# Unused columns that shift where the weights lie against the activations in each partition's memory

## The chip, the cores and the metric

The kernel runs on one core of one Trainium2 chip. Time is device time in microseconds (us), the median of three runs. The kernel computes one decoder layer for 256 tokens; nothing is exchanged with other cores.

## The reference, cut to what matters

```python
def hybrid_layer(x, ...):                      # x: (1, 256, 1024) float32
    h = rmsnorm(x, norm_mix_g)
    proj = h @ w_in                            # 1024 -> 3*512 + 512 + 2*1024
    q, k, v, u_pool, gate_logits = jnp.split(proj, ...)
    q = apply_partial_rotary(rmsnorm(heads(q), q_norm_g), pos)
    k = apply_partial_rotary(rmsnorm(heads(k), k_norm_g), pos)
    attn = moba_attention(q, k, heads(v))      # 256 tokens are one block: causal attention, 8 heads of 64
    pooled = multiscale_pool_mixer(u_pool, w_pool, pool_scale)
    gates = jax.nn.sigmoid(gate_logits + b_gate)
    mixed = gates[:, :, 0] * (attn @ w_branch_attn) + gates[:, :, 1] * (pooled @ w_branch_pool)
    x = x + mixed @ w_out
    h2 = rmsnorm(x, norm_ffn_g)
    up = causal_depthwise_conv(h2 @ w_up, conv_w, conv_b)     # 1024 -> 2*2816
    gate, val = jnp.split(up, 2, axis=-1)
    return x + (jax.nn.silu(gate) * val) @ w_down             # 2816 -> 1024
```

## The kernel before, in words

**Three products for one.** Each float32 operand is split into a part rounded to float32r (`hi`, written by `high`, an ACT copy) and the rest (`lo`, written by `low`, a subtraction on DVE, in the feed-forward activations on POOL). Each 128x128 block of a product is then three TensorE matmuls: hi by hi, hi by lo, lo by hi (`mm3`, lines 92 to 94; `down`, lines 640 to 642; `project`, line 283). Every matmul has a stationary operand of 128 columns, which a weight load (PEld) brings in, and a moving operand that is streamed past it.

**Two forms.** From the pooling projection on (`ps_u`, `ps_g`, `ps_m`, `ps_bp`, `ps_ba`, `ps_out`, `ps_up`, `ps_d`) the weights are stationary and the activations, all 256 tokens, are moving: 128x256. In `project`, which makes q, k and v, it is the other way round: 128 tokens of the activations are stationary, and 512 columns of the weights move. The kernel issues 352, 352 and 352 matmuls for `ps_up`, 176 three times for `ps_d`, 128 three times for `ps_g`, 64 three times for `ps_out`, 32 three times each for `ps_u`, `ps_bp` and `ps_ba`, and 4 three times for `ps_m`. Between them stand a few float32 matmuls: transposes (`ps_tq`, `ps_tk`, `ps_p`), scores and values of the attention (`ps_s`, `ps_o`) and the statistics (`ps_n`, lines 243 and 254).

**How the weights come.** `load` brings chunks of 1 MB into four `raw` buffers, on SyncE's queue; `ahead` splits them into four `whi` and four `wlo` buffers some pieces before use; `chunk` hands them to the matmuls. All engines keep the order of the program.

**Where things lie.** A partition's memory is handed out pool after pool: first the constants (pool `const`), then `raw`, `whi`, `wlo`, and then `act`, whose first tile is `xq`: 8 columns of norm weights, then x and the q weights. Behind it in `act` stand `xhi`/`hhi`, `xlo`/`hlo`, `qkT`/`mh`, `vn`/`ml`, `poolh`, `pooll`, `ath` and `atl`, and behind those a pool for temporaries (`ah`, `al`, `u`, `cv` in the feed-forward part). A weight buffer has 8192 bytes in a partition, a stationary slice 512 bytes, a moving slice 1024 bytes (2048 in `project`), so every slice of the weights begins at the same place modulo 512, and every slice of the split activations too. In the built program of before, all of `raw`, `whi` and `wlo` begin at byte 448 modulo 512, and the tiles of `act` behind `xq`, with `ah` and `al`, at 480.

Of the kernel before, what the change touches and what calls it, by code (L numbers as in the profile page):

```python
# [8 lines left out]
F32 = mybir.dt.float32  # L9
# [5 lines left out]
P = 128  # L15
S = 256
NT = S // P
D = 1024
KD = D // P
H = 8  # L20
DH = 64
AW = H * DH
# [30 lines left out]
FFN_AHEAD = 6  # L53
KREADY = 0
FIRST = 2
XCUTS = (1, 2, 4, 6, 8)


@with_exitstack
def hybrid_layer_kernel(ctx: ExitStack, tc: tile.TileContext, xq_d, par_d, wkv_d, wpg_d,  # L60
                        wpool_d, wba_d, wbp_d, wout_d, wup_d, wdn_d, out_d):
    nc = tc.nc

    const = ctx.enter_context(tc.tile_pool(name="const", bufs=1))
# [3 lines left out]
    act = ctx.enter_context(tc.tile_pool(name="act", bufs=1))  # L68
# [109 lines left out]
    nc.vector.memset(ones, 1.0)  # L178


    xq_all = act.tile([P, KD + KD * (S + AW)], F32, name="xq")
    gmix = xq_all[:, 0:KD]
    xq = xq_all[:, KD:].rearrange("p (k c) -> p k c", c=S + AW)
    xT = xq[:, :, 0:S]
# [5 lines left out]
    cut = 0  # L190
    for k in XCUTS:
        end = KD + k * (S + AW)
# [17 lines left out]

    ident = const.tile([P, P], F32, name="ident")
    make_identity(nc, ident)
    mhalf = const.tile([P, H], F32, name="mhalf")
    nc.gpsimd.memset(mhalf, -0.5)
    mask = const.tile([P, 3, P], F32, name="mask")
# [215 lines left out]
    def scores(hp):  # L431
        ps = ps2.tile([P, 2, 512], F32, tag="ps2", name=f"ps_s{hp}")
        for j in range(2):
            rows = slice(j * DH, (j + 1) * DH)
            nc.tensor.matmul(ps[:, j, P:3 * P], qT[rows, hp, P:S], kT[rows, hp, :], start=True, stop=True)
            nc.tensor.matmul(ps[:, j, 0:P], qT[rows, hp, 0:P], kT[rows, hp, 0:P], start=True, stop=True)
        sm = tmp.tile([P, 2, 3 * P], F32, tag="big", bufs=4, name=f"sm{hp}")
        nc.vector.tensor_tensor(sm, ps[:, :, 0:3 * P],
                                mask.rearrange("p a b -> p (a b)")[:, None, :].to_broadcast([P, 2, 3 * P]), ALU.add)
        mx = tmp.tile([P, 2, 2], F32, tag="mx", name=f"mx{hp}")  # L440
        for t in (1, 0):
            nc.vector.tensor_reduce(mx[:, t, :], sm[:, :, TOK[t]], axis=AX.X, op=ALU.max)
        nc.vector.tensor_scalar(mx, mx, -(DH ** -0.5), None, op0=ALU.mult)
        sums = tmp.tile([P, 2, 2], F32, tag="sums", name=f"sums{hp}")
        for j in range(2):
            for t in (1, 0):
                nc.scalar.activation(sm[:, j, TOK[t]], sm[:, j, TOK[t]], AF.Exp, bias=mx[:, t, j:j + 1],
                                     scale=DH ** -0.5, accum_out=sums[:, t, j:j + 1])
        rs = tmp.tile([P, 2, 2], F32, tag="rs", name=f"rs{hp}")
        nc.vector.reciprocal(rs, sums)  # L450
        for t in (1, 0):
            n = TOK[t].stop - TOK[t].start
            nc.gpsimd.tensor_tensor(sm[:, :, TOK[t]], sm[:, :, TOK[t]],
                                    rs[:, t, :, None].to_broadcast([P, 2, n]), ALU.mult)
        later(4, weigh, hp, sm)
# [46 lines left out]
    for n in range(2 * KD):  # L502
        if n >= FIRST and (n - FIRST) % 4 == 0:
            scores((n - FIRST) // 4)
        if n == 10:
# [275 lines left out]
```

## Time and profile before

| what | value |
|---|---|
| median of 3 runs | 347.75 us (347.67 to 347.77) |
| the profiled execution | 347.8 us, of which 346.0 us is the span from the first instruction to the last |
| PE (matmuls) | busy 340.3 us, 98% |
| PEld (weight loads) | 329.3 us, 95% |
| DVE, ACT, POOL | 259.3 us (75%), 198.1 us (57%), 89.4 us (26%) |
| granted TensorE clock, mean | 0.998 |

The span and what lies outside it (1.8 us) make up the execution's time. Matmuls overlap in the records: one is listed with 280 ns, while the next starts 0.11 to 0.12 us after it. The distance from start to start, called the pitch below, is what a matmul costs in a stream of them.

### The profile page before, as it was taken

What the parts mean: (1) busy time and instruction counts of PE and PEld (TensorE: products, weight loads), DVE (VectorE), ACT (ScalarE), POOL (GpSimd) and SP (SyncE); (2) the same over time, 40 slices, a digit from 0 to 9 for tenths busy, and PEclk for the clock granted to TensorE, in tenths of its full rate; (3) what the DMA queues carried; (4) which work ended last, traced back from release to release, by engine and by line L of the source; (5) the groups of instructions that cost most, each with busy time, mean ns of one, the idle gap of its engine ahead of it and who ended that gap; (6) DMA issues with size and microseconds to landing.
All of it is one profiled execution on the core that took longest, in us unless ns stands there. A gap on an engine that the chain in (4) does not pass through costs nothing.

```text
span 346.0 us, 6726 instructions
## 1 busy us (share of the span) xinstructions
PE 340.3 (98%) x2736; PEld 329.3 (95%) x2736; DVE 259.3 (75%) x411; ACT 198.1 (57%) x319; POOL 89.4 (26%) x103
## 2 busy tenths in 40 slices
PE   8999999999999999999999999999999999999995
PEld 7887899999999999999999999999999999999995
DVE  4969889787587585798699977777777777768633
ACT  4956534634748944776467755555556464646420
POOL 1007991112202034123142212121212121221230
PEclk9999999999999999999999999999999999999999
DMA  7985642365272560574257557364646455641003
GB/s 273 421 333 211 217 168 108 150 214 213 86 265 90 230 215 30 172 275 170 116 197 268 183 206 243 122 244 131 236 137 228 145 223 168 209 180 54 0 2 121
DMA packets 10414, 62.76 MB, mean 181 GB/s; under 512 B 1168, under 2 KB 2448, under 8 KB 3472
## 3 DMA queue, kind: packets, MB, share of 16 engines
q1 hardware_dynamic: 10160, 62.01, 49.9%
q8 instruction: 21, 0.34, 0.4%
q10 hardware_dynamic: 224, 0.33, 0.3%
q14 instruction: 9, 0.07, 0.1%
HBM read 61.29 MB, written 1.05 MB: 180 GB/s over the span
## 4 chain that ended last, share of the span: by engine, by line
PE 90%; DMA 5%; DVE 3%; ACT 1%; issue 0%; POOL 0%; SPq 0%; ACTq 0%
PE ps_up L94 12%; PE ps_up L92 12%; PE ps_up L93 12%; PE ps_d L642 6%; PE ps_d L641 6%; PE ps_d L640 6%; PE ps_g L92 5%; PE ps_g L94 4%; PE ps_g L93 4%; DMA raw_k<-in_wkv 3%; PE ps_v L283 3%; PE ps_out L92 2%; PE ps_out L94 2%; PE ps_out L93 2%; PE ps_bp L92 1%; DMA xq<-in_xq 1%
## 5 line engine op out<-in xcount | busy, mean ns | idle before, releaser
L92 PE MATMUL ps_up<-hhi,hi_up 128*128 128x256 f32 x352 | 98.5, 280 | 0.0
L94 PE MATMUL ps_up<-hhi,lo_up 128*128 128x256 f32 x352 | 98.4, 279 | 0.0
L93 PE MATMUL ps_up<-hlo,hi_up 128*128 128x256 f32 x352 | 98.3, 279 | 0.0
L94 PEld LDWEIGHTS ps_up<-hhi,lo_up 128*128 128x128 f32 x352 | 66.2, 188 | 0.2 <-DVE lo_up L84 0.2
L92 PEld LDWEIGHTS ps_up<-hhi,hi_up 128*128 128x128 f32 x352 | 66.2, 188 | 0.0
L93 PEld LDWEIGHTS ps_up<-hlo,hi_up 128*128 128x128 f32 x352 | 66.2, 188 | 0.0
L84 DVE TENSOR_TENSOR lo_up<-raw_up,hi_up 128x1024 fp32r<-128x1024 f32 x44 | 54.5, 1242 | 6.1 <-ACT hi_up L80 6.1
L641 PE MATMUL ps_d<-al,hi_dn 128*128 128x256 f32 x176 | 49.1, 279 | 0.0
L640 PE MATMUL ps_d<-ah,hi_dn 128*128 128x256 f32 x176 | 49.1, 279 | 0.0
L642 PE MATMUL ps_d<-ah,lo_dn 128*128 128x256 f32 x176 | 49.1, 279 | 0.0
L623 POOL TENSOR_TENSOR c_v<-c_g,c_v 128x256 f32<-128x256 f32 x22 | 16.2, 736 | 121.4 <-DVE c_v L606 121.4
L80 ACT ACTIVATE hi_up<-raw_up 128x1024 fp32r<-128x1024 f32 x44 | 44.9, 1044 | 0.0
L92 PE MATMUL ps_g<-xhi,hi_g 128*128 128x256 f32 x128 | 36.5, 285 | 0.0
L93 PE MATMUL ps_g<-xlo,hi_g 128*128 128x256 f32 x128 | 35.7, 279 | 0.0
L94 PE MATMUL ps_g<-xhi,lo_g 128*128 128x256 f32 x128 | 35.7, 279 | 0.0
L80 ACT ACTIVATE ah<-c_v 128x256 fp32r<-128x256 f32 x22 | 9.2, 419 | 45.7 <-POOL c_v L623 45.7
L641 PEld LDWEIGHTS ps_d<-al,hi_dn 128*128 128x128 f32 x176 | 33.1, 188 | 0.0
L642 PEld LDWEIGHTS ps_d<-ah,lo_dn 128*128 128x128 f32 x176 | 33.1, 188 | 0.0
L640 PEld LDWEIGHTS ps_d<-ah,hi_dn 128*128 128x128 f32 x176 | 33.1, 188 | 0.0
L611 DVE TENSOR_TENSOR u_v<-ps_up,R 128x256 f32<-128x256 f32 x22 | 9.3, 422 | 25.7 <-PE ps_up L94 25.6
L84 DVE TENSOR_TENSOR lo_dn<-raw_dn,hi_dn 128x1024 fp32r<-128x1024 f32 x22 | 27.8, 1264 | 0.4 <-ACT hi_dn L80 0.4
L647 POOL TENSOR_TENSOR al<-c_v,ah 128x256 fp32r<-128x256 f32 x22 | 22.8, 1038 | 11.6 <-ACT ah L80 11.6
(182 smaller groups left out, 806.7 us busy)
## 6 DMA issues: line engine op xcount, KB each, us to landing
raw_up<-in_wup SPq DMA_DIRECT2D x22, 1024.0 KB, 4.8
raw_dn<-in_wdn SPq DMA_DIRECT2D x11, 1024.0 KB, 4.7
raw_g<-in_wpg SPq DMA_DIRECT2D x8, 1024.0 KB, 4.8
raw_o<-in_wout SPq DMA_DIRECT2D x4, 1024.0 KB, 4.7
xq<-in_xq SPq DMA_DIRECT2D x3, 768.0 KB, 7.4
raw_v<-in_wkv SPq DMA_DIRECT2D x2, 1024.0 KB, 14.0
raw_p<-in_wpg SPq DMA_DIRECT2D x2, 1024.0 KB, 6.2
raw_bp<-in_wbp SPq DMA_DIRECT2D x2, 1024.0 KB, 4.7
```

The costliest lines, as they stand in the source:

```text
L80: nc.scalar.activation(hi, src, AF.Copy, scale=scale)
L84: nc.vector.tensor_tensor(lo, src, hi.bitcast(F32), ALU.subtract)
L92: nc.tensor.matmul(out, sh, mh, start=start, stop=False, **kw)
L93: nc.tensor.matmul(out, sh, ml, start=False, stop=False, **kw)
L94: nc.tensor.matmul(out, sl, mh, start=False, stop=stop, **kw)
L283: nc.tensor.matmul(pt[t], sx[:, k, t * P:(t + 1) * P], wx[:, sl], start=k == 0 and sx is xhi and wx is hi, stop=k == KD - 1 and wx is lo)
L611: nc.vector.tensor_tensor(u, ps[:, 0:S], R2, ALU.mult)
L623: nc.gpsimd.tensor_tensor(uc[1], g[1], uc[1], ALU.mult)
L640: nc.tensor.matmul(o, hi[:, sl], acch[i], start=first, stop=False, skip_group_check=True)
L641: nc.tensor.matmul(o, hi[:, sl], accl[i], start=False, stop=False, skip_group_check=True)
L642: nc.tensor.matmul(o, lo[:, sl], acch[i], start=False, stop=i == KF - 1, skip_group_check=True)
L647: nc.gpsimd.tensor_tensor(accl[i], act_i, acch[i].bitcast(F32), ALU.subtract)
```

## The change

A tile `home` of 56 columns (224 bytes) is added to the constants, and POOL writes one column of it, so that it exists. The tile `xq` becomes 72 columns (288 bytes) longer in front, and everything that uses it begins behind these. No other line differs, and no engine but POOL has another instruction.

In the changed program `raw`, `whi` and `wlo` begin at byte 160 modulo 512 instead of 448 (224 bytes further on). The two additions together are 512 bytes, so x, the q weights inside `xq`, all of `act` behind it and the temporaries keep their place modulo 512 (480 for the split activations). The activations therefore stand 320 bytes behind the weights, modulo 512, where they stood 32 behind them. The constants that are allotted after `home` (`mhalf`, `mask`, `rcnt`, `R1`, `R2`, `diag` and the small statistics) move by the 224 bytes as well; `ones`, `par` and `ident` stay.

```diff
@@ -53,6 +53,8 @@
 FFN_AHEAD = 6
 KREADY = 0
 FIRST = 2
+HOME = 56
+LEAD = 72
 XCUTS = (1, 2, 4, 6, 8)
@@ -178,7 +180,7 @@
-    xq_all = act.tile([P, KD + KD * (S + AW)], F32, name="xq")
+    xq_all = act.tile([P, LEAD + KD + KD * (S + AW)], F32, name="xq")[:, LEAD:]
     gmix = xq_all[:, 0:KD]
     xq = xq_all[:, KD:].rearrange("p (k c) -> p k c", c=S + AW)
@@ -210,6 +212,8 @@
     ident = const.tile([P, P], F32, name="ident")
     make_identity(nc, ident)
+    home = const.tile([P, HOME], F32, name="home")
+    nc.gpsimd.memset(home[:, 0:1], 0.0)
     mhalf = const.tile([P, H], F32, name="mhalf")
     nc.gpsimd.memset(mhalf, -0.5)
```

## Rows read from the trace of the kernel before

**Rows 1.** Busy time of each engine by stage (us; in brackets instructions).
```profile
core 0: us, PE busy (x) PEld busy (x) DVE busy (x) ACT busy (x) POOL busy (x), PEclk, DMA share, GB/s
0.00:30.00 30.00, 28.27 (x120) 22.97 (x120) 21.40 (x36) 20.30 (x30) 4.25 (x12) 1.00 0.82 322
30.00:41.00 11.00, 11.00 (x48) 8.88 (x49) 10.90 (x15) 4.77 (x7) 10.61 (x11) 1.00 0.60 203
...
56.00:116.00 60.00, 59.90 (x511) 57.24 (x510) 46.34 (x78) 37.52 (x77) 9.70 (x8) 1.00 0.46 163
...
161.00:186.00 25.00, 24.97 (x212) 24.71 (x212) 21.13 (x35) 14.57 (x24) 6.87 (x7) 1.00 0.41 139
186.00:342.00 156.00, 156.00 (x1339) 155.99 (x1338) 112.12 (x170) 83.56 (x125) 33.77 (x38) 1.00 0.47 166
```
**Rows 2.** The chain that ended last, at its two ends (start, length).
```profile
4.95 12.00 DMA raw_k<-in_wkv
...
29.93 11.20 PE ps_v L283 x47
41.13 0.12 PE ps_u L92
...
342.08 0.13 PE ps_d L642
342.20 0.02 issue
342.23 0.42 DVE xq L703
```
**Rows 3.** Groups of matmuls by form: count, busy us, mean ns of one.
```profile
L92 PE MATMUL ps_up<-hhi,hi_up 128*128 128x256 f32 x352 | 98.5, 280 | 0.0
...
L640 PE MATMUL ps_d<-ah,hi_dn 128*128 128x256 f32 x176 | 49.1, 279 | 0.0
...
L92 PE MATMUL ps_g<-xhi,hi_g 128*128 128x256 f32 x128 | 36.5, 285 | 0.0
```
**Rows 4.** Timeline of PE in the feed-forward part, first and last matmul of a stretch.
```profile
300.03 0.28 PE L92 MATMUL ps_up<-hhi,hi_up 128*128 128x256 f32 x1
...
341.91 0.28 PE L642 MATMUL ps_d<-ah,lo_dn 128*128 128x256 f32 x1
```
**Rows 5.** Busy time in the same stretch (361 matmuls, two of them begun before it).
```profile
300.03:341.91 41.88, 41.88 (x361) 41.88 (x360) 26.97 (x44) 17.84 (x28) 8.53 (x10) 1.00 0.20 69
```
**Rows 6.** Timeline of PE in the v projection (128x512).
```profile
36.78 0.63 PE L283 MATMUL ps_v<-hi_v,xhi 128*128 128x512 f32 x2
37.24 0.63 PE L283 MATMUL ps_v<-hi_v,xlo 128*128 128x512 f32 x2
37.71 0.63 PE L283 MATMUL ps_v<-lo_v,xhi 128*128 128x512 f32 x2
38.18 0.40 PE L283 MATMUL ps_v<-hi_v,xhi 128*128 128x512 f32 x1
```
**Rows 7.** The chain again: float32 work between the products (start, length).
```profile
46.75 0.87 PE ps_tq L319 x8
...
165.05 0.43 PE ps_n L254 x2
```
**Rows 8.** Groups of POOL in the first 26 us.
```profile
L246 POOL TENSOR_TENSOR rtok<-var_n,mhalf 128x2 f32<-128x2 f32 x1 | 0.7, 711 | 22.7 <-DVE var_n L245 22.7
...
L214 POOL MEMSET mhalf<- 128x8 f32 x1 | 0.1, 104 | 0.0
```
**Rows 9.** Waits of PE from 30 us to the end (us in total, times, longest).
```profile
PE ps_v L283 <- DVE qg_q L296: 0.2, 1, 0.2
```
**Rows 10.** Timeline of PE: statistics with one moving column.
```profile
22.96 0.36 PE L243 MATMUL ps_n<-ones,vn 128*128 128x1 f32 x2
...
23.18 0.48 PE L283 MATMUL ps_k<-hi_k,xhi 128*128 128x512 f32 x1
```
**Rows 11.** Groups of weight loads (count, busy us, mean ns of one).
```profile
L92 PEld LDWEIGHTS ps_up<-hhi,hi_up 128*128 128x128 f32 x352 | 66.2, 188 | 0.0
...
L319 PEld LDWEIGHTS ps_tq<-ident,qg_q 128*128 128x128 f32 x8 | 0.9, 140 | 0.0
...
L243 PEld LDWEIGHTS ps_n<-ones,vn 128*128 128x128 f32 x4 | 0.6, 190 | 0.1
```

## The prediction

> **What bounds the kernel now.** I read the busy time by stage first [rows 1]. PE is busy in all of every stretch from 30 to 342 us; DVE comes next with 72% of the long feed-forward stretch (112.12 of 156 us), 77% of 56 to 116 us and 85% of 161 to 186 us, and the DMA engines are busy about half of the time. Then the chain that ended last [rows 2]: until 29.93 us it is made of transfers and of work on several engines, from there to 342.20 us almost all PE, and one addition on DVE and the output's transfers follow. So about 312 us of the span are a queue of matmuls that waits for hardly anything, and only two things can shorten it: fewer matmuls, or a smaller pitch. The change leaves the matmuls as they are.
>
> The pitch therefore decides, and the durations in the groups [rows 3] don't give it, since 280 ns overlaps the next two. From the first to the last matmul of a stretch [rows 4], 41.88 us with 361 matmuls of which two began before it [rows 5], 359 pitches make 41.88 / 359 = 0.1167 us. At the granted clock of 1.00, which is 2.4 GHz, that is 280 cycles for 256 columns; the columns alone would be 256 / 2.4 = 106.7 ns. The long stretch with transfers at 166 GB/s and the last one at 69 GB/s [rows 1, 5] have the same pitch (156 us for 1337 to 1339 matmuls is 116.5 to 116.7 ns), so what costs the 10 ns is not other engines or transfers: it lies in what PE itself does. In the v projection six matmuls of 512 columns go from 36.78 to 38.18 us [rows 6], 233 ns each against 213 for the columns alone. That is the same share.
>
> **Which rows show PE without the loss.** The eight transposes of 46.75 us take 0.87 us, 109 ns each; they move 128 columns in float32, and the two matmuls of line 254 with 256 columns take 0.43 us, 215 ns each [rows 7]. That is two cycles a column (106.7 and 213.3 ns) to within 3 ns, while a weight load of 128 columns goes on beside them. So PE streams without loss where the moving operand is read at half the rate, and loses 24 cycles in 280 where it is read at one column each cycle beside a weight load. Both reads come from the same partitions, the one from weights, the other from activations, and their distance modulo 512 is the same for every matmul of this kernel. It is that distance which the change sets.
>
> **The change part by part.**
>
> *The memset of `home`.* One column more on POOL, before `mhalf`: 0.10 us by the row of the memset of eight columns; POOL's next work that anything waits for, `rtok`, comes after 22.7 us of idle time [rows 8]. Cost nothing; without that cover 0.10 us.
>
> *Memory and transfers.* 512 bytes more in a partition. The transfers have the same pieces, the same number and the same order, into other addresses. The start, until 29.93 us, is taken as unchanged: its transfers fill 0.82 of the DMA engines [rows 1], and no size changes. I bound it at 0.1 us either way, the size of the memset's row.
>
> *DVE, ACT and POOL.* A split reads and writes inside the weight buffers alone, or inside the activations alone, so the operands of these instructions keep their distances, but for the ones that read `R1`, `R2` or `mask`. None of these engines is the bound: from 30 us on PE waits for them for 0.2 us in all, at one place [rows 9]. Price nothing, up to what they have free.
>
> *The distance of the two reads.* This is the term that matters, and the trace of before has one distance only, so its price is bounded by rows. The matmuls of the 128x256 form are 3 x (352 + 176 + 128 + 64 + 3 x 32 + 4) = 2460, the first three counts by [rows 3]. All come after 41 us, on the path. The upper bound of the gain is the pitch of the transposes, 109 ns: 7.7 ns x 2460 = 18.9 us, and 48 matmuls of v from 233 to 215 ns, 0.9 us: 19.8 us. The lower bound of the gain is nothing, and a loss isn't excluded (below). Between them stands a floor that I take for the forecast: the statistics with one moving column [rows 10] have almost nothing to stream, and still the two from 22.96 us take until 23.18, 111 to 112 ns each with the digits of the rows: that is what a fresh float32 stationary operand costs by itself. Their weight loads last 190 ns, like the 188 of the products, where those of the transposes last 140 [rows 11], so the products belong to this row and not to the transposes'. If the loss goes, the pitch falls to 111.3 ns, not 109: (116.7 - 111.3) x 2460 = 13.3 us. For v I count nothing, since DVE is busy for 10.90 of the 11.00 us there [rows 1] and what follows waits for its splits.
>
> *What would be late next.* An iteration of the feed-forward part has 72 matmuls, 8.4 us now and 8.0 us then; DVE's 72% becomes 75%, and in 161 to 186 us 85% becomes 89%. DMA would carry 174 instead of 166 GB/s, and it moved 322 in the first 30 us [rows 1]. So the gain would be kept.
>
> Sum: 347.8 (the profiled execution, 0.05 above the median) - 13.3 = 334.5 us.
>
> **The rivals.**
>
> *The loss does not come from the distance* (no change, 347.7 us). For it: the loss is the same share, 24 of 280 and 20 of 233, in two forms in which the roles of weights and activations are exchanged and in which the weight load fills quite different shares of the pitch. If the two reads got into each other's way, a load that comes half as often should cost half as much per column, and here it costs the same. So it may be that moving 4 bytes each cycle is what the read port can't quite keep up with, and then no address helps. Against it: the distance has the same size in both forms, 32 bytes one way and the other, so the equal share may be a coincidence of two stalls. The Trainium skill speaks for this rival: SBUF — State Buffer, section Who interferes with whom, gives PE two independent read ports, one for the moving operand and one for weight loads, and says that PE never waits on anyone; by it the new distance would change nothing. Its page TensorE: Matmul & The Clock Gate, section Back-to-back issue gap, gives N / 2.4 + 2.5 ns, which is 109.2 ns for 256 columns; the measured 116.7 ns [rows 4, 5] doesn't agree, so something that these pages don't have costs 7.5 ns here; were all of it given back, the gain would be 7.5 ns x 2460 = 18.4 us.
>
> *The new distance is worse* (slower). The mechanism is the same as in the forecast, and the other sign: where 32 bytes make the two streams meet for 24 cycles of a matmul, 320 bytes may make them meet for longer. It is slower as soon as the pitch rises by 0.7 us / 2460 = 0.3 ns. Half as much loss again (5 ns) is 12.3 us, 360 us; the whole again, 24.6 us, 372 us. Against it: nothing in the rows but that there is less room below the columns' time than above; for it, that no row shows another distance.
>
> *Only a part of the loss goes.* A third of it (8 cycles, 3.3 ns) is 8.2 us, 339.6 us. I count it with the forecast.
>
> **How the numbers follow.** The loss goes wholly or in part: 0.55, with its own range from 328.0 (the upper bound of the gain) to 342. No effect: 0.31. Worse: 0.14. A measurement of this kernel tells 0.2% (0.7 us) from no change; the forecast's cases lie beyond that, so faster 0.55, same 0.31, slower 0.14. The prediction is that of the likeliest, 334.5 us. The range goes from 328.0 to 349.0: it takes in the forecast and no effect, and leaves out the slower case and gains above the bound, some 16 in 100.
>
> **What would show it.** Right: the 128x256 matmuls start 111 to 112 ns after one another in all stages, equally with and without transfers; the stretch from the first `ps_u` to the last `ps_d` is 13 us shorter, and the start until about 30 us is as before. Wholly removed: 109 ns. No effect: 116.7 ns again, to the digit. Worse: above 117 ns. The prediction is also wrong if the pitch falls and idle time of PE before `ps_up` or `ps_g` takes its place, released by DVE's `lo` or ACT's `hi`: then the supply of split weights is the bound. It would be a surprise if the 512-column matmuls changed and the 256-column ones did not, since both sets of reads have the same distance.

## The result, and the profile after

The changed kernel takes 350.38 us (350.32 to 350.42, 4 runs) against 347.76 us (347.67 to 347.84, 4 runs) before: ratio 1.0072, 95% interval 1.006 to 1.0084. (The ratios in this document leave out executions over 1.5% above the fastest of their kernel.) It is slower, by 2.6 us, where 13.3 us less were forecast. The profiled execution took 350.36 us with a span of 348.6 us, 2.6 us longer than before.

Busy time by stage of the changed kernel (as [rows 1]; the program is the same in each stage):

```profile
core 0: us, PE busy (x) PEld busy (x) DVE busy (x) ACT busy (x) POOL busy (x), PEclk, DMA share, GB/s
30.00:41.00 11.00, 11.00 (x48) 8.89 (x49) 10.90 (x15) 4.77 (x7) 10.61 (x11) 1.00 0.58 197
56.00:116.00 60.00, 59.90 (x508) 57.26 (x507) 46.10 (x78) 37.27 (x77) 9.69 (x8) 1.00 0.45 163
116.00:161.00 45.00, 45.00 (x382) 44.37 (x381) 34.54 (x54) 29.61 (x51) 12.07 (x15) 1.00 0.50 175
186.00:342.00 156.00, 156.00 (x1327) 156.00 (x1326) 111.51 (x168) 84.59 (x126) 34.36 (x38) 1.00 0.45 163
```

PE is as full as before, at the same clock, and gets fewer matmuls done: 1327 in the 156 us from 186 us on, where there were 1339 [rows 1]. Two of the 1327 began before the stretch, so 156 us / 1325 is 117.7 ns; from the starts in that stream, with more digits, the pitch is 117.78 ns, and before it was 116.67. The v projection, in which the weights move, has as many matmuls in its 11 us as it had.

The two ends of the chain that ended last (as [rows 2]):

```profile
29.86 11.20 PE ps_v L287 x47
...
344.63 0.13 PE ps_d L646
...
344.78 0.42 DVE xq L707
```

PE's part begins at 29.86 (29.93 before) and ends 2.55 us later than before, and the v projection takes the same 11.20 us. The loss lies in the 2460 matmuls of the 128x256 form: 1.11 ns x 2460 = 2.7 us. No wait has taken it: from 30 us on PE waits for 0.2 us in all, as in [rows 9].

One place of the changed kernel is not slower but faster. Timeline of PE, between two pieces of float32 work:

```profile
74.15 0.28 PE L95 MATMUL ps_g<-xlo,hi_g 128*128 128x256 f32 x1
...
76.30 0.28 PE L96 MATMUL ps_g<-xhi,lo_g 128*128 128x256 f32 x1
```

From 74.15 to 76.30 us 19 matmuls start: 2.15 / 19 = 113 ns each. The same two operands at the same distance go at 117.8 ns in the streams ahead of it and behind it. And in the kernel before, by its starts, one such short stream (`ps_m` and `ps_g`, 88.09 to 91.75 us) goes at 118 ns, where all the others go at about 116.7. The distance alone does not set the pitch; the experiments below come back to this.

### The profile page after: what moved, and what is told of

The parts are those of the page before. It is cut to its first block, busy times and chain, and to the rows that moved or that the text cites. A ratio compares the mean times of both kernels' runs of the same rounds, so it can differ in the third digit from the quotient of the medians.

```text
span 348.6 us, 6727 instructions
## 1 busy us (share of the span) xinstructions
PE 342.4 (98%) x2736; PEld 331.2 (95%) x2736; DVE 259.6 (74%) x411; ACT 198.0 (57%) x319; POOL 89.8 (26%) x104
## 4 chain that ended last, share of the span: by engine, by line
PE 90%; DMA 4%; DVE 3%; ACT 1%; issue 0%; POOL 0%; SPq 0%; ACTq 0%
PE ps_up L96 12%; PE ps_up L95 12%; PE ps_up L94 12%; PE ps_d L646 6%; PE ps_d L645 6%; PE ps_d L644 6%; PE ps_g L94 5%; PE ps_g L95 4%; PE ps_g L96 4%; DMA raw_k<-in_wkv 3%; PE ps_v L287 3%; PE ps_out L96 2%; PE ps_out L95 2%; PE ps_out L94 2%; PE ps_bp L94 1%; PE ps_ba L96 1%
```

## Experiments

The theory after the result: the pitch depends on the distance of the two reads, and the new distance is a little worse. Rivals: the place of the weights in the partition, or the moved constants, cost the time.

**One half of the change at a time.** `e1_home_only` is the changed kernel without the columns in front of x:

```diff
-LEAD = 72
+LEAD = 0
```

> Only the tile behind the constants is kept: weights and activations both move by 224 bytes, and their distance is 32 bytes as before (weights at 160, activations at 192 modulo 512). Theory A (the distance between the two reads decides): the pitch of the 128x256 matmuls is 116.7 ns as before, and the time 347.8 us. Theory B (the place of the weights itself decides): 117.8 ns and 350.4 us as with the whole change. Theory C (it is the moved constants, R1, R2, mask, read by DVE): also 350.4 us, but the pitch would not show it inside a stream.

`e2_lead_only`: the kernel before with the longer `xq` alone.

```diff
+LEAD = 72
...
-    xq_all = act.tile([P, KD + KD * (S + AW)], F32, name="xq")
+    xq_all = act.tile([P, LEAD + KD + KD * (S + AW)], F32, name="xq")[:, LEAD:]
```

> Only the columns in front of x are kept: the weights stay at 448, the activations go to 256, their distance is 320 as in the whole change. Theory A (distance): 117.8 ns, 350.4 us. Theory B (place of the weights): 116.7 ns, 347.8 us. Theory C (constants): 347.8 us.

Measured, where the kernel before took 347.94 us: `home` alone 348.29 us, ratio 1.0004 (0.9993 to 1.0014); the columns in front of x alone 350.24 us, ratio 1.0061 (1.0046 to 1.0076). PE in 150 us of the feed-forward part, first with `home` alone, then with the columns alone:

```profile
186.00:336.00 150.00, 150.00 (x1288) 1.00 0.47 169
```
```profile
186.00:336.00 150.00, 150.00 (x1276) 1.00 0.46 168
```

The pitch from the starts is 116.66 and 117.78 ns. In this part, with the distance of 32 bytes, the pitch is that of before although the weights lie elsewhere, and with 320 it is that of the change, with the weights and the constants where they were. Both rivals fall.

One stretch with `home` alone is an exception. PE in two stretches of 18 us, and the two starts between them where a gap stands:

```profile
166.00:184.00 18.00, 18.00 (x155) 1.00 0.43 152
187.00:205.00 18.00, 18.00 (x157) 1.00 0.72 264
```
```profile
184.28 0.28 PE L95 MATMUL ps_up<-hlo,hi_up 128*128 128x256 f32 x1
184.46 0.39 PE L96 MATMUL ps_up<-hhi,lo_up 128*128 128x256 f32 x1
```

From the starts it is 117.8 ns in the first stretch and 116.66 in the second, at the same distance of 32 bytes and in the same part of the kernel; between them one matmul starts 0.18 us behind the one before it. So 117.8 ns is not a property of 320 bytes alone.

**All distances.** `e3_bursts` adds bursts of 24 matmuls (21 in the last 16) to the kernel before, behind the last product:

```diff
...
+    def burst(name, o, m, n=8):
+        b = bank(f"ps_x{name}")
+        for k in range(n):
+            st = slice(o + k * 256, o + k * 256 + P)
+            mv = slice(m + k * 256, m + k * 256 + S)
+            mm3(b[:, 0:S], (bh[:, st], bl[:, st]), (hh2[:, mv], hl2[:, mv]), k == 0, k == n - 1)
...
+    for d in range(32):
+        burst(LETTERS[d // 16] + LETTERS[d % 16], 4 * d, 0)
+    for d in range(16):
+        burst("c" + LETTERS[d], 8 * d, 8 * d, 7)
```

> The kernel before, with 48 bursts of 128x256 matmuls added behind the last product; their results are not used. In the first 32 the slices of the weights begin 0, 16, 32, ... 496 bytes further on, in steps of 16, and the activations stay, so that the distance falls from 32 in the same steps; in the last 16 both move together in steps of 32 bytes. Theory A: the pitch differs between the first 32 bursts, is 116.7 ns in the first one and 117.8 ns in the one 224 bytes on (distance 320), and is 116.7 in all of the last 16. If some distance has no loss, its burst shows 109 to 112 ns. Theory B: the first 32 differ, and the last 16 differ in the same way. Rival that distance matters only a little: all bursts lie between 116 and 119 ns.

Busy time of PE from the start of a burst to the start of the next, for the distances (modulo 512) 32, 288, 256, 208, 192, 144 and 64 in that order, and last for 14 of the bursts in which both operands move together:

```profile
343.58:346.41 2.83, 2.83 (x26) 1.00 0.51 145
388.93:391.73 2.80, 2.80 (x27) 1.00 0.02 6
394.60:397.48 2.88, 2.88 (x27) 1.00 0.00 0
403.16:405.98 2.82, 2.82 (x26) 1.00 0.00 0
405.98:408.71 2.73, 2.73 (x27) 1.00 0.03 6
414.37:417.25 2.88, 2.88 (x26) 1.00 0.00 0
428.68:431.51 2.83, 2.83 (x27) 1.00 0.00 0
434.31:468.75 34.44, 34.44 (x297) 1.00 0.01 1
```

A length divided by 24 is the pitch with a burst's beginning in it; from the starts of its later matmuls it is 117.9, 116.7, 119.6, 117.85, 113.3, 120.35 and 117.75 ns. So the pitch goes from 113.3 to 120.4 ns over the bursts. In 14 of 16 pairs of bursts that lie 256 bytes apart it is equal to 0.1 ns: the distance counts modulo 256, where 320 is 64. The two unequal pairs are 32 and 288 bytes (117.9 and 116.7 ns) and 16 and 272 (117.2 and 119.85). So the first burst, at the kernel's own 32 bytes, did not show the 116.7 ns that was expected of it; the bursts that move together, at 32 bytes too, do. The 14 bursts in which both operands move together take 34.44 / (14 x 21) = 117.1 ns with their beginnings, 116.5 to 116.8 without: the place makes no difference. No distance in steps of 16 bytes shows the 111 ns that I had taken.

**Which reads, and how many.** `e4_sizes`, bursts again:

```diff
...
+    def swapped(name, o, n=4):
...
+            st = slice(k * 256, k * 256 + P)
+            mv = slice(o + (k % 3) * 512, o + (k % 3) * 512 + 512)
+            mm3(b, (hh2[:, st], hl2[:, st]), (bh[:, mv], bl[:, mv]), k == 0, k == n - 1)
...
+    def sized(name, o, cols, moving, n=8):
...
+            st = slice(o + k * 256, o + k * 256 + cols)
+            mv = slice((k % 6) * 256, (k % 6) * 256 + moving)
+            mm3(b[0:cols, 0:moving], (bh[:, st], bl[:, st]), (hh2[:, mv], hl2[:, mv]), k == 0, k == n - 1)
```

> The kernel before, with bursts added behind the last product: 16 of 128x512 with the weights moving (distance in steps of 32 bytes), then at two distances (32 and 320) seven with 128, 192, ... 512 moving columns and three with 32, 64 and 96 stationary columns; their results are not used. If the loss belongs to a weight load's reads, it is a fixed number of ns for each matmul, falls with fewer stationary columns, and the 512-column matmuls at some distances differ from 233 ns. If it belongs to the moving reads alone, it stays 9.4% of the columns' time from 256 to 512 columns, and is the same with 32 stationary columns and at all distances.

Timeline of the burst with 128 moving columns, then PE's busy time over whole bursts (24 matmuls): 320, 384 and 512 moving columns, and 32 stationary columns, all at distance 32, and 32 stationary columns at 320:

```profile
387.38 0.28 PE L92 MATMUL ps_zaa<-hhi,hi_dn 128*128 128x128 f32 x1
...
388.72 0.28 PE L92 MATMUL ps_zaa<-hhi,hi_dn 128*128 128x128 f32 x1
```
```profile
394.92:398.44 3.52, 3.52 (x26) 1.00 0.02 5
398.44:402.60 4.16, 4.16 (x26) 1.00 0.00 0
407.55:413.15 5.60, 5.60 (x25) 1.00 0.00 0
413.15:416.02 2.87, 2.87 (x25) 1.00 0.00 0
447.81:450.55 2.74, 2.74 (x25) 1.00 0.00 0
```

With 128 columns 12 matmuls take 1.34 us, 112 ns, and with 192 it is 111.6 ns too: the floor of [rows 10] is borne out, since the number of moving columns doesn't change it. Above, the loss grows with the moving columns: 10 ns at 256, 146.7 - 133.3 = 13 ns at 320, 173.3 - 160 = 13 ns at 384, 233.3 - 213.3 = 20 ns at 512. With fewer stationary columns it goes both ways: at distance 32, 96, 64 and 32 of them go at 116.6, 117.7 and 120 ns, and at 320 all three settle at 113.4. And the 512-column form depends on the distance as well, 226.8 to 234.9 ns over its 16 bursts; the two distances of the kernels both happen to give 233. So neither of the two expectations holds whole. The loss has to do with both operands, since their distance moves it, but it is not a fixed price of a weight load. That the two reads get into each other's way is the explanation that I draw from this; no run shows the reads themselves.

**Which data type.** `e8_fine` steps the distance by 4 bytes around the best one, and repeats the bursts in bfloat16 and float32 (`plain`: 24 matmuls of one stationary and one moving operand, with eight distances 32 bytes apart):

```diff
...
+    for d in range(16):
+        burst("a" + LETTERS[d], 16 + d, 0)
...
+    for d in range(8):
+        plain("a" + LETTERS[d], 16 * d, w16, a16, S)
+    for d in range(8):
+        plain("b" + LETTERS[d], 8 * d, bh.bitcast(F32), hh2.bitcast(F32), S)
+    for d in range(8):
+        plain("c" + LETTERS[d], 16 * d, w16, a16, 512)
```

> The kernel before with bursts behind the last product, whose results are not used: 16 with the weights 64 to 124 bytes on in steps of 4, around the best distance; then eight distances each of bfloat16 with 256 moving columns, float32 with 256, and bfloat16 with 512. If the two reads meet because float32r takes 4 bytes each cycle, bfloat16 and float32 show one pitch at all distances (bfloat16 107 to 112 ns and 213 to 216, float32 two passes of 215), and only float32r depends on the distance. If the meeting is of the two operands whatever their width, bfloat16 depends on it too. In steps of 4 bytes: if lines of 16 bytes matter, groups of four bursts agree; if some distance has no loss, it shows 111 to 112 ns.

PE's busy time over all eight bursts of bfloat16 (192 matmuls of 256 columns), then over all eight of float32 (192 matmuls, each recorded as two passes of 256 columns):

```profile
387.13:408.10 20.97, 20.97 (x195) 1.00 0.01 2
408.10:490.98 82.88, 82.88 (x387) 1.00 0.00 1
```

20.97 / 192 = 109.2 ns and 82.88 / 384 = 215.8 ns, the same in every burst to 0.1 ns: no dependence on these eight distances. Of the three types only float32r has it, the one that moves four bytes in about one cycle (256 columns at 113.3 ns are 272 cycles at 2.4 GHz). In steps of 4 bytes, one burst each, the pitch of float32r goes back and forth between 113.4 and 120 ns, without groups of four; 113.35 is the lowest of all.

**Another distance in the kernel.** `e5_lead40` and `e7_lead28` are `e2_lead_only` with other numbers, `e6_home24_lead104` is the change with other numbers:

```diff
...
-HOME = 56
-LEAD = 72
+HOME = 24
+LEAD = 104
```

> The kernel before with 40 columns (160 bytes) in front of x and nothing behind the constants: distance 192, the best of the bursts (113.3 ns). If the bursts carry over to the kernel: pitch 113.3 ns, (116.7 - 113.3) x 2460 = 8.2 us less, 339.6 us. If in the kernel another engine or the supply of weights takes over: the pitch falls, PE shows idle time before ps_up or ps_g, and the time stays above 342 us. If the bursts say nothing about the kernel: 347.8 us.

> Both additions of the change with other sizes, 96 bytes behind the constants and 416 in front of x: weights at 32, activations at 480 as in the kernel before and after, distance 448. By a period of 256 bytes, as the bursts show it, this is distance 192 again: 113.3 ns, 339.6 us. If the period is 512 in the kernel, it is another number than with 40 columns in front of x.

> The kernel before with 28 columns (112 bytes) in front of x: distance 144, the worst of the bursts (120.35 ns). If the bursts carry over: 3.7 ns x 2460 = 9.1 us more, 356.9 us. If they don't: 347.8 us.

Measured, where the kernel before took 347.95 us: distance 192, 342.35 us, ratio 0.982 (0.9791 to 0.985); distance 448, 343.24 us, ratio 0.985 (0.982 to 0.9879); distance 144, 349.91 us, ratio 1.0055 (1.0033 to 1.0076). The best two are faster than both kernels, but by 5 to 6 us and not by 8, and the worst one is slower by 2 us and not by 9. PE in two stretches with distance 192, `ps_out` to `ps_up` and the feed-forward part, then with 448 `ps_bp` to `ps_up` and the feed-forward part:

```profile
135.12:156.67 21.55, 21.55 (x191) 1.00 0.56 197
186.00:336.00 150.00, 150.00 (x1326) 1.00 0.47 169
```
```profile
120.00:156.00 36.00, 36.00 (x308) 1.00 0.50 172
186.00:336.00 150.00, 150.00 (x1326) 1.00 0.47 170
```

In the feed-forward part both run at 113.3 ns. From 120 to 156 us the first runs at 113.3 and the second at 117.8 (36.00 us for 306 starts), though the distances are the same modulo 256; and several streams between two pieces of float32 work run at 117.8 in both. At distance 144 the feed-forward part runs at 117.3 and not at the 120 of its burst. So something beside the distance takes part, and I suspected what lies between the streams. With distance 192 about half of the 2.75 us above the expected 339.6 comes from such streams (by the starts, 312 matmuls between 47 and 118 us at 117.8 ns instead of 113.3: 1.4 us); 0.7 us are waits for splits from 150 to 190 us.

The times of single executions differ in the same manner. Two of the six with distance 192 took 348.2 us at a granted clock of 1.00, so the gain is not there in every execution. The 5.9 us between them and the others are what 4.45 ns more for each of the 1326 matmuls of the feed-forward row would cost. The kernel before took 347.75 to 348 us in nine of its 17 executions in this comparison and 348.6 to 350.45 in eight; the slowest is what all 2460 matmuls at 117.8 ns would give (347.75 + 2.7 us). Both are estimates: no trace of such an execution was kept. With distance 144 three of ten took 351.0 to 351.7 us.

**The start of a stream.** `e9_history` repeats a burst twelve times at each of four distances, behind one to three float32 matmuls of another width each time:

```diff
...
+    for name, o in (("a", 0), ("b", 56), ("c", 24), ("d", 36)):
+        for i in range(12):
+            reset = bank(f"ps_r{name}{LETTERS[i]}")
+            for _ in range(1 + i % 3):
+                nc.tensor.matmul(reset[:, 0:1 + 9 * i], ones, ones[:, 0:1 + 9 * i], start=True, stop=True)
+            burst(name + LETTERS[i], o, 0)
```

> The kernel before with 48 bursts behind the last product, twelve at each of the distances 32, 320, 192 and 144, whose results are not used. Ahead of each burst stand one to three float32 matmuls of ones with another number of columns each time, so that a burst begins with another timing between the weight loads and the streams. If the distance alone sets the pitch: twelve equal numbers at each distance, 116.7, 117.8, 113.3 and 117.3 or 120. If distance and the timing at the start of a stream set it together, as 113.3 and 117.8 ns in one kernel at distance 192 let suppose: two or more values at some distances, and 192 shows both 113.3 and 117.8.

PE's busy time over bursts: two at distance 32, two at 320, two at 192, one at 144:

```profile
343.44:346.24 2.80, 2.80 (x27) 1.00 0.49 139
356.46:359.29 2.83, 2.83 (x26) 1.00 0.00 0
382.64:385.47 2.83, 2.83 (x27) 1.00 0.00 0
389.41:392.13 2.72, 2.72 (x26) 1.00 0.03 6
421.83:424.55 2.72, 2.72 (x27) 1.00 0.00 0
425.00:427.83 2.83, 2.83 (x26) 1.00 0.00 0
460.56:463.44 2.88, 2.88 (x27) 1.00 0.00 0
```

From the starts: at 32, five bursts at 116.7 to 116.9 and seven at 117.8 to 118.0; at 320, eleven at 117.8 and one at 113.3; at 192, seven at 113.3 to 113.6 and five at 117.8; at 144, all at 119.6 to 120.0. Once settled, after at most five matmuls, each burst at 32, 320 and 192 bytes keeps its value to its end. So a burst of `e3_bursts` or `e8_fine` shows one rhythm of its distance and not all of them.

`e10_after_reset` does the same in the changed kernel, ahead of each iteration of the feed-forward part:

```diff
+            reset = bank(f"ps_r{i}")
+            for _ in range(1 + i % 3):
+                c = 1 + 9 * (i % 12)
+                nc.tensor.matmul(reset[:, 0:c], ones, ones[:, 0:c], start=True, stop=True)
             ps = [up_tile(w, 0, i)]
```

> The changed kernel (distance 320) with one to three float32 matmuls of ones ahead of each iteration of the feed-forward part from the third on, of another number of columns each time; their results are not used, and they cost time of their own, so only the pitch within an iteration counts. If the distance alone sets the pitch in the kernel: 117.8 ns in all twenty iterations. If the timing at the start of a stream takes part, as in the bursts: most iterations 117.8 ns, some 113.3 ns, and nothing between for a whole iteration.

PE's busy time in four iterations, from the second matmul to a little behind the last start (70 pitches and 0.23 us):

```profile
175.99:184.15 8.16, 8.16 (x74) 1.00 0.62 241
184.61:193.09 8.48, 8.48 (x74) 1.00 0.66 247
256.03:264.20 8.17, 8.17 (x74) 1.00 0.40 145
264.65:273.13 8.48, 8.48 (x74) 1.00 0.67 232
```

Three of the twenty run at 113.3 ns, the others at 117.8, none between. In the changed kernel too the distance leaves the stream two rhythms, and the one it falls into at its start stays. What is put ahead does not alone decide which: `i = 3` and `i = 15` have the same float32 matmuls ahead of them, and so have `i = 2` and `i = 14`, and of each pair one runs at 113.3 and the other at 117.8.

## Why the prediction was wrong

- **The bound, and where a gain or loss would show: right.** PE is full from 30 us on in both traces, the matmuls are the same, and the difference is pitch x 2460, with the start, the v projection and the waits unchanged to 0.1 us.
- **That the distance of the two reads takes part: right.** e1 and e2 show it against the place and the constants, and e8 that of three data types it is float32r alone. What the prediction did not have is that one distance allows two pitches.
- **The step that failed:** "If the loss goes, the pitch falls to 111.3 ns". The range of the price was fair (nothing to 7.7 ns, and a loss not excluded), but I then put the new distance at its good end, 5.4 ns less, and no row spoke for 320 bytes rather than for another distance. Measured, it is 1.1 ns more: the streams of the changed kernel fall into a rhythm of 117.8 ns, all but one, where nearly all streams of the kernel before fall into one of 116.7. The 111 ns themselves were right as a floor, with 128 or 192 moving columns, but no 256-column stream of float32r came below 113.3 ns.
- **The rivals.** "The new distance is worse" was the case, at 0.14, with 5 ns given for half of the loss again where it is 1.1. "The loss does not come from the distance" fell with e1, e2 and e3. Its argument, that the same share in two forms speaks against a meeting of the reads, was a coincidence of two distances: e4 has 226.8 to 234.9 ns for the 512-column form. What the Trainium skill has beside it (SBUF — State Buffer, Who interferes with whom: PE's read port for the moving operand and its port for weight loads are independent) does not let expect what float32r shows, where the distance between PE's own two operands moves the pitch by up to 7 ns; the measurement decides. For bfloat16 and float32 e8 shows nothing against it, and for bfloat16 the Trainium skill's N / 2.4 + 2.5 (TensorE: Matmul & The Clock Gate, Back-to-back issue gap) agrees: 109.2 ns for 256 columns and 215.8 for 512, as measured in e8.
- **The sign.** That 0.55 stood on the faster side came from reading "there is a loss, and the change sets what causes it" as "the change takes it away". With bursts from 113.3 to 120.4 ns, a kernel at 116.7 is better than most of them. On which side it comes out hangs on the setting, for which no row spoke: the same change with other numbers (`e6_home24_lead104`) gained 4.7 us.

Open: why a float32r stream loses cycles at all, why the loss grows with the moving columns and not with the stationary ones, what repeats every 256 bytes, and what at a stream's start chooses the rhythm. Open, too, is why the kernel's feed-forward part runs at 117.3 ns at distance 144, when all twelve bursts of `e9_history` at 144 run at 119.6 to 120.0. The runs show that these things are so, and not the mechanism.

## What to carry to other kernels

Where TensorE is full, compare the distance between starts with the time of the columns alone, in each form and each stream apart: a steady excess in float32r is worth a sweep over where the operands lie, which one run with bursts behind the kernel's own work gives for dozens of distances. A price that a change can have on either side of today's is not a gain until a row shows that very setting. And check the best distance in the kernel itself, stream by stream, since what stands ahead of a stream can put it into another rhythm.

## What the runs showed that I had not expected

A stream of equal float32r matmuls has two steady rhythms at one distance (113.3 and 117.8 ns at 192 and at 320 bytes, 116.7 and 117.8 at 32), chosen at its start or behind a gap and kept for as long as the stream lasts, which in the feed-forward part is over a thousand matmuls. So one execution of a kernel shows one of the times that its distance allows: the kernel before, at its 32 bytes, reached 350.45 us, which is the time of the changed one.
